# Padding the activation slots and weight ring of a hybrid decoder layer so that matmul operands start in many alignments

## The chip, the cores and the metric

The kernel runs on one core of a Trainium2 chip. The time is the device time of one execution of the whole layer, in microseconds. Before the change the median of two runs was 1518.17 us (1517.32 to 1519.03).

## What is computed

One layer of a decoder for 256 tokens with 2048 features, all in float32. Cut to what matters:

```python
def hybrid_mixer(h, w_in, mla_q_norm, mla_w_q_up, mla_kv_norm, mla_w_kv_up,
                 swa_sinks, rel_table, w_o_mla, w_o_swa, w_out):
    c_q, c_kv, k_r, q_s, k_s, v_s, gates = jnp.split(h @ w_in, offsets, axis=-1)
    q = (rms_norm(c_q, mla_q_norm) @ mla_w_q_up).reshape(B, S, MLA_HEADS, MLA_NOPE_DIM + MLA_ROPE_DIM)
    kv = (rms_norm(c_kv, mla_kv_norm) @ mla_w_kv_up).reshape(B, S, MLA_HEADS, MLA_NOPE_DIM + MLA_V_DIM)
    ...
    o_a = mla_attention(q[..., :MLA_NOPE_DIM], q_rope, kv[..., :MLA_NOPE_DIM], k_rope, kv[..., MLA_NOPE_DIM:])
    o_b = swa_attention(q_s, k_s, v_s, swa_sinks, rel_table)
    g = jax.nn.sigmoid(gates.astype(jnp.float32)).reshape(B, S, N_BRANCHES, D_MODEL)
    merged = g[:, :, 0] * (o_a @ w_o_mla).astype(jnp.float32) + g[:, :, 1] * (o_b @ w_o_swa).astype(jnp.float32)
    return merged.astype(h.dtype) @ w_out

def reference(x, ...):
    h = rms_norm(x, norm_mix_pre[l])
    y = hybrid_mixer(h, w_in[l], ...)
    x = x + rms_norm(y, norm_mix_post[l])
    h = rms_norm(x, norm_ffn_pre[l])
    y = conv_ffn(h, ffn_w_up[l], ffn_conv_w[l], ffn_conv_b[l], ffn_w_down[l])
    return x + rms_norm(y, norm_ffn_post[l])
```

`conv_ffn` multiplies by `w_up` (2048 x 11264), runs a causal convolution of width 3 and a gated GELU, and multiplies by `w_down` (5632 x 2048). Most of the work is in the large products with w_in (2048 rows, 7488 columns), w_o_mla, w_o_swa, w_out, w_up and w_down.

## The kernel before

**Splitting into high and low parts.** Each float32 factor is stored as two float32r parts, high and low, whose sum is the number. A product takes three matmuls (`mm3`, lines 142 to 145): high activation with high weight, high with low, low with high. The activation is the stationary operand (128 x 128, loaded into the array), the weight is the moving one (up to 512 columns that stream past it).

**Large products** go through `gemm` (lines 147 to 173). It keeps two accumulators of 128 tokens x 512 columns in PSUM and walks over the rows of the weight, in chunks of two tiles of 128 rows (1024 numbers a partition; for 320 columns also two tiles, for 256 four). `wchunk` (lines 101 to 120) fetches a chunk: SyncE issues the load into a raw buffer (three in the ring), ScalarE writes its high part (line 118), VectorE subtracts and writes the low part (line 119). The ring has five buffers for high parts and five for low parts, of 1024 numbers, 4096 bytes a partition. For some chunks `own` gives another pool (`px`, `p8`) in place of the ring, at the seams of the W_out and FFN stages. So for each chunk of two row tiles and each of two token tiles TensorE runs three matmuls: twelve of 512 columns.

**Activation slots.** Transposed activations lie in slots of 512 numbers (2048 bytes a partition): a pair of row tiles, each with 256 tokens. `slot_a` and `slot_b` (lines 92 and 93) name 16 slots each in the pool `base`: ah0 to ah7 and al0 to al7, bh0 to bh7 and bl0 to bl7. `pair_view` (line 95) picks row tile k: slot k // 2, and 256 numbers from its half. The a slots hold first the normed input (products with w_in), then the merged branches (w_out), then eight of the twelve gated FFN pairs (w_down); the b slots hold the sliding-window output (w_o_swa), the latent-attention output (w_o_mla), and the normed FFN input (w_up). The remaining four FFN pairs, gh8 to gh11 and gl8 to gl11, are tiles of the pool `p7` (line 876).

**Where things lie.** Pools lie one behind the other in a partition; each tile starts at a multiple of 32 bytes. In `base` come the constants, the a slots, seven small tiles of the input norm (ssx, v1, r1s, rh, r1_y, r1_t, r1_u), the b slots, eight small tiles of the latents' norms; then the ring with its raw, high and low buffers; then the pools of the stages.

**Order of the work.** Attention and the convolution run in small steps (`at`, `tick`) that are emitted between the chunks of the large products. Except in the first product, a scheduler in the framework sets the order on each engine; the change touches none of it.

Of the kernel before, what the change touches and what calls it, by code (L numbers as in the profile page):

```python
# [12 lines left out]
F32R = mybir.dt.float32r  # L13
# [28 lines left out]
def trunk_layer(ctx, tc, x, g_mix_pre, g_mix_post, g_ffn_pre, g_ffn_post, w_in, g_q, w_q, g_kv, w_kv,  # L42
# [16 lines left out]
    def sb(pl, shape, name, dt=F32, tag=None, bufs=None):  # L59
        return pl.tile(shape, dt, name=name, tag=tag or name, **({"bufs": bufs} if bufs else {}))  # L60

# [1 line left out]
    ident = sb(base, [P, P], "ident")  # L63
    make_identity(nc, ident)
    ident_r = sb(base, [P, P], "ident_r", F32R)
# [22 lines left out]
    rtab = sb(base, [P, NT, 4, 64], "rtab")  # L88
    sink = sb(base, [P, SH], "sink")

    # activations, transposed, as high and low float32r parts
    slot_a = lambda p, part: sb(base, [P, 512], f"a{part}{p}", F32R)
    slot_b = lambda p, part: sb(base, [P, 512], f"b{part}{p}", F32R)

    def pair_view(tiles):
        return lambda k: tiles[k // 2][:, (k % 2) * 256:(k % 2) * 256 + 256]

# [1 line left out]
    cnt = [0]  # L99

    def wchunk(src, shape, own=None, rawp=None):
        i = cnt[0]
        cnt[0] += 1
        n = int(np.prod(shape))
        raw = rawp.tile([P, 1024], F32, name=f"raw{i}", tag="xraw") if rawp else \
            ring.tile([P, 1024], F32, name=f"raw{i}", tag="raw", bufs=RAW)
        dst = raw[:, :n]
        if len(shape) == 2:
            dst = dst.rearrange("p (a b) -> p a b", a=shape[0])
        elif len(shape) == 3:  # L110
            dst = dst.rearrange("p (a b c) -> p a b c", a=shape[0], b=shape[1])
        if len(shape) == 3:
            for k in range(shape[0]):
                nc.sync.dma_start(dst[:, k], src[:, k])
        else:
            nc.sync.dma_start(dst, src)
        hi, lo = ((own or ring).tile([P, 1024], F32R, name=f"w{part}{i}", tag="w" + part) for part in ("hi", "lo"))
        act.copy(hi[:, :n], raw[:, :n])  # L118
        vec.tensor_tensor(lo[:, :n], raw[:, :n], hi[:, :n].bitcast(F32), op=ALU.subtract)  # L119
        return hi, lo  # L120

    # side work, in small steps that are emitted between the chunks of the large products
    steps = defaultdict(list)
    now = [0]

# [19 lines left out]
        pe.matmul(o, al, bh, start=False, stop=stop)  # L145

    def gemm(xh, xl, w, k0, nk, c0, n, split=False, pre=None, extra=None):
        """tokens x n columns of (activation rows k0.. of w); split: all of token tile 0 first."""
        kc = 1024 // n if n in (256, 512) else 2
        acc = new_acc("g")  # L150
        todo = []
        cuts = [0, 1, 2] + list(range(4, nk + 1, 2)) if pre else list(range(0, nk, kc)) + [nk]
        for ci, (k, ke) in enumerate(zip(cuts[:-1], cuts[1:])):
            kk = ke - k
            src = w[(k0 + k) * P:(k0 + k + kk) * P, c0:c0 + n].rearrange("(a p) n -> p a n", p=P)
            if pre and ci == 0:
                pre(k, ke)
            hi, lo = wchunk(src, [kk, n], *(extra or {}).get(ci, ()))
            if pre and ke < nk:
                pre(ke, cuts[ci + 2])  # L160
            for j in range(kk):
                kt = k + j
                wh, wl = hi[:, j * n:(j + 1) * n], lo[:, j * n:(j + 1) * n]
                for t in range(NT):
                    def go(kt=kt, t=t, wh=wh, wl=wl):
                        mm3(acc[t][:, :n], xh(k0 + kt)[:, t * P:(t + 1) * P],
                            xl(k0 + kt)[:, t * P:(t + 1) * P], wh, wl, kt == 0, kt == nk - 1)
                    if split and t == 1:
                        todo.append(go)
                    else:  # L170
                        go()
            tick()
        return acc, todo

    def rsqrt(v, n, name, pl):
        y = sb(pl, [P, n], f"{name}_y")
        t = sb(pl, [P, n], f"{name}_t")
        u = sb(pl, [P, n], f"{name}_u")
        vec.tensor_scalar(y.bitcast(I32), v.bitcast(I32), -0.5, float(0x5F3759DF), op0=ALU.mult, op1=ALU.add)
        def vyy():  # L180
            if n == 1:
                vec.scalar_tensor_tensor(t, v, y[:, 0:1], y, op0=ALU.mult, op1=ALU.mult)
            else:
                vec.tensor_tensor(t, y, y, op=ALU.mult)
                vec.tensor_tensor(t, t, v, op=ALU.mult)

        # a step of second order, then one of third order
        vyy()
        vec.tensor_scalar(t, t, -0.5, 1.5, op0=ALU.mult, op1=ALU.add)
        vec.tensor_tensor(y, y, t, op=ALU.mult)  # L190
        vyy()
        vec.tensor_scalar(u, t, 0.375, -1.25, op0=ALU.mult, op1=ALU.add)
        vec.tensor_tensor(u, u, t, op=ALU.mult)
        vec.scalar_tensor_tensor(y, u, 1.875, y, op0=ALU.add, op1=ALU.mult)
        return y

    def split_to(hi, lo, src, scale=None):
        """hi + lo = src * scale exactly; src in PSUM or SBUF, scale a number or a [P, 1] column."""
        if scale is None:
            act.copy(hi, src)  # L200
            vec.tensor_tensor(lo, src, hi.bitcast(F32), op=ALU.subtract)
        else:
            act.activation(hi, src, AF.Copy, scale=scale)
            vec.scalar_tensor_tensor(lo, src, scale, hi.bitcast(F32), op0=ALU.mult, op1=ALU.subtract)

# [1 line left out]
    esl, lpool = open_pool("lpool")  # L207
    es0, p0 = open_pool("p0")
    grow = sb(p0, [16, P], "grow")
# [53 lines left out]
    rh = sb(base, [P, NT], "rh")  # L263
    junk = sb(p0, [P, 512], "junk", tag="junk", bufs=2)

    # T5 bias of each head along the distance, with the mask beyond the window
    strip = dram.tile([SH, 384], F32, name="strip")
    relx = sb(lpool, [33, SH], "relx")
    pool.memset(relx[32:33, :], 1.0)
# [24 lines left out]
    r1 = x_norm()  # L294
    es0.close()

# [1 line left out]
    # keys and values run backwards within their blocks, so that the bias is strip[q + column]  # L298
    es1, p1 = open_pool("p1")
    kx = [sb(p1, [P, 2, 384], f"kx{g}", F32R) for g in range(4)]  # L300
    vx = [sb(p1, [P, 4, 2, 64], f"vx{t}", F32R) for t in range(NT)]
# [34 lines left out]
    qx_of, xs_of = {}, {}  # L336

    def swa_q(g, acc):
        """8 heads' queries, high parts beside low parts"""
        qx_of[g] = []  # L340
        for t in range(NT):
            q = sb(p1, [P, 8, 2, 64], f"qx{g}_{t}", F32R, tag="qx", bufs=2)
            a3 = acc[t].rearrange("p (a b) -> p a b", b=64)
            split_to(q[:, :, 0, :], q[:, :, 1, :], a3, r1s[:, t:t + 1])
            qx_of[g].append(q)

    def swa_qT(u):
        """queries of heads 2u, 2u + 1, transposed: high parts above low parts"""
        qx, i = qx_of[u // 4], u % 4
        pt = pst.tile([P, 512], F32R, name=f"xp{u}", tag="t")  # L350
        for j in range(2):
# [5 lines left out]
        xs_of[u] = xt  # L357

    def p_transpose(p, dst, tag):
        """probabilities [q0k0 | q1k0 | q1k1] of a head, transposed: [q1k1 | q0k0 | q1k0]"""  # L360
        pt = pst.tile([P, 512], F32, name=f"pt{tag}", tag="t")
        for j, c in enumerate((2, 0, 1)):
            pe.transpose(pt[:, j * P:(j + 1) * P], p[:, c * P:(c + 1) * P], ident)  # L363
        split_to(dst[0], dst[1], pt[:, 0:384])

    def swa_unit(u, t0):
        """heads 2u, 2u + 1, from step t0 on"""
        g = u // 4
        h0 = 2 * u
        st = {}  # L370
# [51 lines left out]
            p_transpose(st["p"][:, i, :], [w_[:, i, :] for w_ in st["pt"]], f"{u}_{i}")  # L422

        def pv():
            """high V above low V, against the probabilities' high and low parts of both heads"""
            st["po"] = pst.tile([P, 512], F32, name=f"po{u}", tag="t")
            st["o"] = sb(p1, [P, 256], f"o{u}", tag="o", bufs=2)
            v0, v1 = (vx[t][:, g, :, :].rearrange("p a b -> p (a b)") for t in range(NT))
# [25 lines left out]
            at(b + 1 + i // 2, lambda u=4 * g + i: swa_qT(u))  # L454
            swa_unit(4 * g + i, b + 2 + 2 * i)

# [1 line left out]
    cqh = [sb(lpool, [P, 512], f"cqh{i}", F32R) for i in range(2)]  # L458
    cql = [sb(lpool, [P, 512], f"cql{i}", F32R) for i in range(2)]
    ckh = sb(lpool, [P, 512], "ckh", F32R)  # L460
# [26 lines left out]
        return nrm, tr  # L487

    def rope(dst, src, tmp, t, which, nh):
        """dst = rope(src); src, dst [P, nh, 64], tables [cos | cos] and [-sin | sin]"""  # L490
        c = rtab[:, t, which, :]
        s = rtab[:, t, which + 1, :]
        b = lambda ap, n: ap.unsqueeze(1).to_broadcast([P, nh, n]) if nh > 1 else ap.unsqueeze(1)
# [28 lines left out]
    at(now[0] + 2, k_rope)  # L522
    at(now[0] + 3, lambda tr=tr: tr(0))

# [1 line left out]
    ta_d = dram.tile([4, NT, P, 512], F32, name="ta_d")  # L526
    yb_d = dram.tile([4, NT, P, 512], F32, name="yb_d")

# [16 lines left out]
    drain()  # L545
    es1.close()

# [1 line left out]
    es2, p2 = open_pool("p2")  # L549
    CQH, CQL = pair_view(cqh), pair_view(cql)  # L550
    CKH, CKL = pair_view([ckh]), pair_view([ckl])
# [3 lines left out]
    xr_of = {}  # L555

    def q_rope4(f, t0):
        """rope queries of heads 4f.., transposed, high above low, from step t0 on"""
        st = {}

        def mms(t):
# [28 lines left out]
        at(t0 + 4, lambda: tr(1))  # L590

    def mla_unit(u, t0):
        """heads 2u, 2u + 1, from step t0 on"""
        h0 = 2 * u
        st = {}

# [113 lines left out]
    es2.close()  # L710
    esl.close()

# [1 line left out]
    es3, p3 = open_pool("p3")  # L714
    mth = [slot_a(p, "h") for p in range(8)]
    mtl = [slot_a(p, "l") for p in range(8)]
# [34 lines left out]
        for p in range(2):  # L751
            at(now[0] + 1 + p, lambda p=2 * j + p, ld=ld: m_cols(p, ld))

# [1 line left out]
    gpost = sb(p6, [P, D], "gpost", tag="gp")  # L755
    pool.dma_start(gpost, g_mix_post.partition_broadcast(P))
    yg = [[sb(p6, [P, 512], f"yg_{t}_{j}", tag="f" + "ab"[t], bufs=4) for j in range(4)] for t in range(NT)]
# [64 lines left out]
            for t in range(NT):  # L822
                y_evac(acc, b, t)

# [1 line left out]
    first_extra = {0: (p8,)} | {i + 1: (px,) for i in range(EXTRA)}  # L826
    first_extra[EXTRA + 2] = (None, p8)
    resid(1)
# [1 line left out]
    GH, GL = pair_view(gT[0]), pair_view(gT[1])  # L830

    def conv_cols(sa, k, i, slot):
        """conv, gelu and gate of channels 128k.., into ktile slot"""
        w0, w1, w2, cb_ = (cvT[:, 44 * q + k:44 * q + k + 1] for q in range(4))
        pt = pst.tile([P, 512], F32, name=f"fT{k}", tag="t")
        for q in range(2):
# [14 lines left out]
        split_to(GH(slot), GL(slot), uu)  # L851

    def ffn_up(c, slot0, first=False):
        """channels 512c.., into ktiles slot0.."""
        sa = [[None, None], [None, None]]

        def evac(acc, q):
# [136 lines left out]
```

## Time and profile before

| | |
|---|---|
| median of two runs | 1518.17 us |
| profiled execution, first to last instruction | 1515.5 us |
| difference between the two | 2.7 us |
| TensorE matmuls | 7347, busy 1496.3 us |
| weight loads into the array (PEld) | 7347, busy 1246.4 us |
| VectorE busy | 940.8 us |
| ScalarE busy | 800.4 us |
| bytes moved by DMA | 285.46 MB, mean 188 GB/s |

Busy times of one engine can overlap those of another. PE is the matmul itself, PEld the load of its stationary operand, which runs beside the matmul before it. A matmul's recorded duration includes the passage through the array and overlaps the next one, so a mean duration of 390 ns does not mean one matmul every 390 ns; the time from start to start gives the pace. In a row of the groups stand line, engine, operation, output and inputs (moving first, stationary second), shape, count, then busy time in us and mean ns of one, then idle time before them.

### The profile page before, as it was taken

How to read it: one execution, taken by the hardware profiler on the slowest of the kernel's cores; microseconds unless marked ns; L12 is line 12 of the kernel's file. 1: busy time of each engine (PE TensorE's matmuls, PEld its weight loads, DVE VectorE, ACT ScalarE, POOL GpSimd, SP SyncE). 2: the span in 40 equal slices, each digit the busy share in tenths (PEclk: the TensorE clock that was granted, in tenths of full speed). 3: DMA queues.
4: the chain of work that ended last, by engine and by line, in shares of the span. 5: the costliest groups of instructions: out<-in, count | busy, mean ns of one | idle time of the engine just before them, and what ended most of it. 6: DMA issues, size and time to landing. Idle time of an engine off the chain costs nothing.

```text
span 1515.5 us, 20149 instructions
## 1 busy us (share of the span) xinstructions
PE 1496.3 (99%) x7347; PEld 1246.4 (82%) x7347; DVE 940.8 (62%) x1607; ACT 800.4 (53%) x1289; POOL 66.8 (4%) x114
## 2 busy tenths in 40 slices
PE   8999999999999999999999999999999999999997
PEld 6888878888898887888788888888888888888887
DVE  5688884444666764565676666666544476666755
ACT  6588874344555553444565555555434455555542
POOL 2122200000000002000000000000000000000000
PEclk9999999999999999999999999999999999999999
DMA  7776556666655558765655665555566655665553
GB/s 236 215 177 164 164 162 182 208 203 207 181 152 168 162 160 292 254 217 185 199 174 179 196 190 183 184 183 186 185 193 189 193 185 178 189 192 182 179 194 113
DMA packets 160803, 285.46 MB, mean 188 GB/s; under 512 B 18419, under 2 KB 33893, under 8 KB 160448
## 3 DMA queue, kind: packets, MB, share of 16 engines
q1 hardware_dynamic: 154736, 264.81, 55.2%
q0 software_dynamic: 5968, 19.36, 5.0%
q8 instruction: 58, 0.95, 0.2%
q14 instruction: 41, 0.34, 0.1%
HBM read 277.79 MB, written 6.34 MB: 187 GB/s over the span
## 4 chain that ended last, share of the span: by engine, by line
PE 92%; DVE 2%; DMA 2%; ACT 2%; issue 1%; SPq 0%; DVEq 0%; ACTq 0%
PE accg L143 27%; PE accg L145 27%; PE accg L144 27%; DMA raw<-in_w_in_dram 2%; PE fT L838 1%; DVE wlo L119 1%; DMA raw<-in_w_o_mla_dram 1%; PE mpo L679 1%; PE ms L645 1%; ACT whi L118 1%; PE qn L610 1%; PE qn L609 1%; PE qn L608 1%; ACT p L405 0%; PE pt L363 0%
## 5 line engine op out<-in xcount | busy, mean ns | idle before, releaser
L119 DVE TENSOR_TENSOR wlo<-raw,whi 128x1024 fp32r<-128x1024 f32 (+2 forms) x501 | 609.1, 1217 | 496.5 <-ACT whi L118 495.9
L118 ACT CAST whi<-raw 128x1024 fp32r<-128x1024 f32 (+2 forms) x501 | 522.9, 1045 | 603.8 <-PE accg L145 512.6
L143 PE MATMUL accg<-whi,bh 128*128 128x512 f32 x960 | 378.1, 394 | 0.0
L145 PE MATMUL accg<-whi,bl 128*128 128x512 f32 x960 | 374.4, 390 | 0.0
L144 PE MATMUL accg<-wlo,bh 128*128 128x512 f32 x960 | 373.7, 389 | 0.0
L143 PE MATMUL accg<-whi,ah 128*128 128x512 f32 (+2 forms) x896 | 348.7, 390 | 0.4 <-ACT whi L118 0.4
L144 PE MATMUL accg<-wlo,ah 128*128 128x512 f32 (+2 forms) x896 | 345.8, 386 | 0.5 <-DVE wlo L119 0.5
L145 PE MATMUL accg<-whi,al 128*128 128x512 f32 (+2 forms) x896 | 344.8, 385 | 0.0
L145 PEld LDWEIGHTS accg<-whi,bl 128*128 128x128 f32 x960 | 180.2, 188 | 38.5
L144 PEld LDWEIGHTS accg<-wlo,bh 128*128 128x128 f32 x960 | 180.4, 188 | 36.1
L143 PEld LDWEIGHTS accg<-whi,bh 128*128 128x128 f32 x960 | 180.3, 188 | 35.7
L145 PEld LDWEIGHTS accg<-whi,al 128*128 128x128 f32 x896 | 168.7, 188 | 35.6
L144 PEld LDWEIGHTS accg<-wlo,ah 128*128 128x128 f32 x896 | 168.8, 188 | 34.4 <-DVE wlo L119 1.6
L143 PEld LDWEIGHTS accg<-whi,ah 128*128 128x128 f32 x896 | 168.8, 189 | 33.4 <-ACT whi L118 1.3
L143 PE MATMUL accg<-whi,gh 128*128 128x512 f32 (+1 forms) x104 | 39.2, 377 | 0.0
L144 PE MATMUL accg<-wlo,gh 128*128 128x512 f32 (+1 forms) x104 | 38.8, 373 | 0.0
L145 PE MATMUL accg<-whi,gl 128*128 128x512 f32 (+1 forms) x104 | 38.4, 374 | 0.0
L405 ACT ACTIVATE p<-p,nm 128x128 f32<-128x128 f32 x64 | 28.3, 445 | 5.8 <-DVE nm L396 5.8
L838 PEld LDWEIGHTS fT<-ident,f 128*128 128x128 f32 x176 | 21.8, 139 | 5.8
L838 PE MATMUL fT<-ident,f 128*128 128x128 f32 x176 | 26.3, 272 | 0.0
L842 ACT ACTIVATE cc<-fT,cvT 128x256 f32<-128x256 f32 x44 | 24.2, 550 | 0.0
L143 PEld LDWEIGHTS accg<-whi,gh 128*128 128x128 f32 x104 | 19.6, 188 | 4.1 <-ACT gh L200 0.8
(304 smaller groups left out, 1284.7 us busy)
## 6 DMA issues: line engine op xcount, KB each, us to landing
raw<-in_ffn_w_up_dram SPq DMA_DIRECT2D x176, 512.0 KB, 4.0
raw<-in_w_in_dram SPq DMA_DIRECT2D x111, 512.0 KB, 4.4
raw<-in_ffn_w_down_dram SPq DMA_DIRECT2D x88, 512.0 KB, 3.7
raw<-in_w_o_swa_dram SPq DMA_DIRECT2D x32, 512.0 KB, 3.7
raw<-in_w_o_mla_dram SPq DMA_DIRECT2D x32, 512.0 KB, 4.6
raw<-in_w_out_dram SPq DMA_DIRECT2D x32, 512.0 KB, 3.7
raw<-in_mla_w_q_up_dram SPq DMA_DIRECT2D x48, 128.0 KB, 2.6
bias<-strip POOLq DMA_DIRECT2D x16, 256.0 KB, 4.1
```

What stands on the lines that cost most here:

```text
L118: act.copy(hi[:, :n], raw[:, :n])
L119: vec.tensor_tensor(lo[:, :n], raw[:, :n], hi[:, :n].bitcast(F32), op=ALU.subtract)
L143: pe.matmul(o, ah, bh, start=start, stop=False)
L144: pe.matmul(o, ah, bl, start=False, stop=False)
L145: pe.matmul(o, al, bh, start=False, stop=stop)
L405: act.activation(pb[:, i, a:b], pb[:, i, a:b], AF.Exp, bias=st["nm"][:, i, t:t + 1], accum_out=st["sm"][:, i, t:t + 1])
L608: pe.matmul(o, wh, ch(k), start=k == 0, stop=False)
L609: pe.matmul(o, wh, cl(k), start=False, stop=False)
L610: pe.matmul(o, wl, ch(k), start=False, stop=k == nk - 1)
L645: pe.matmul(o, w, v_, start=n == 0, stop=False)
L838: pe.transpose(pt[:, q * 256 + t * P:q * 256 + (t + 1) * P], sa[t][q][:, i * P:(i + 1) * P], ident)
L842: act.activation(cc, a, AF.Identity, scale=w2, bias=cb_)
```

## The change

The slots are allocated 8 numbers (32 bytes) wider, and the program uses 512 numbers of them: in the high slots from the start, in the low slots from number 4, 16 bytes in. High and low chunks of the ring are allocated 8 numbers wider and their first 1024 are used; chunks with a pool of their own stay as they are. So the slots and ring chunks behind each other start 2080 and 4128 bytes apart, where it was 2048 and 4096. Comments and docstrings are dropped; the number of instructions, their shapes and their order in the source are the same.

```diff
-    # activations, transposed, as high and low float32r parts
-    slot_a = lambda p, part: sb(base, [P, 512], f"a{part}{p}", F32R)
-    slot_b = lambda p, part: sb(base, [P, 512], f"b{part}{p}", F32R)
+
+
+    def slot(name, p, part):
+        o = 4 if part == "l" else 0
+        return sb(base, [P, 512 + 8], f"{name}{part}{p}", F32R)[:, o:o + 512]
+
+    slot_a = lambda p, part: slot("a", p, part)
+    slot_b = lambda p, part: slot("b", p, part)
...
-        hi, lo = ((own or ring).tile([P, 1024], F32R, name=f"w{part}{i}", tag="w" + part) for part in ("hi", "lo"))
+        hi, lo = ((own or ring).tile([P, 1024 + (0 if own else 8)], F32R, name=f"w{part}{i}", tag="w" + part)[:, 0:1024]
+                  for part in ("hi", "lo"))
```

## The prediction

> **What bounds the kernel now.** I read the page first: busy shares, the clock by slices, the chain that ended last.
>
> ```profile
> span 1515.5 us, 20149 instructions
> PE 1496.3 (99%) x7347; PEld 1246.4 (82%) x7347; DVE 940.8 (62%) x1607; ACT 800.4 (53%) x1289; POOL 66.8 (4%) x114
> ...
> PEclk9999999999999999999999999999999999999999
> ...
> PE 92%; DVE 2%; DMA 2%; ACT 2%; issue 1%; SPq 0%; DVEq 0%; ACTq 0%
> ...
> raw<-in_ffn_w_up_dram SPq DMA_DIRECT2D x176, 512.0 KB, 4.0
> ```
>
> TensorE is busy for 99% of the span, its clock is granted in full everywhere, and 92% of the chain is matmuls. Then I read the waits, to see whether anything feeds TensorE late.
>
> ```profile
> ACT whi L118 <- PE accg L145: 512.6, 335, 3.5
> DVE wlo L119 <- ACT whi L118: 495.9, 389, 4.2
> ...
> ACT whi L118 <- DMA raw<-in_w_o_mla_dram: 27.2, 14, 4.3
> ```
>
> ScalarE, which writes the high part of each weight chunk, waits 512.6 us for matmuls that give a ring chunk back; for a load it waits a twentieth of that. The ring is full most of the time. So the bound is the pace at which one matmul follows another. Next I read the groups by form, for how many matmuls there are of which size.
>
> ```profile
> L143 PE MATMUL accg<-whi,bh 128*128 128x512 f32 x960 | 378.1, 394 | 0.0
> L145 PE MATMUL accg<-whi,bl 128*128 128x512 f32 x960 | 374.4, 390 | 0.0
> L144 PE MATMUL accg<-wlo,bh 128*128 128x512 f32 x960 | 373.7, 389 | 0.0
> L143 PE MATMUL accg<-whi,ah 128*128 128x512 f32 x800 | 320.6, 401 | 0.4 <-ACT whi L118 0.4
> L144 PE MATMUL accg<-wlo,ah 128*128 128x512 f32 x800 | 317.7, 397 | 0.5 <-DVE wlo L119 0.5
> L145 PE MATMUL accg<-whi,al 128*128 128x512 f32 x800 | 316.8, 396 | 0.0
> ...
> L143 PE MATMUL accg<-whi,gh 128*128 128x512 f32 x88 | 34.7, 395 | 0.0
> L144 PE MATMUL accg<-wlo,gh 128*128 128x512 f32 x88 | 34.3, 390 | 0.0
> L145 PE MATMUL accg<-whi,gl 128*128 128x512 f32 x88 | 33.9, 391 | 0.0
> ```
>
> There are 3 x (960 + 800 + 88) = 5544 matmuls of 512 columns. The surprise is the mean: 401, 397, 396 ns with the a slots as stationary operand, but 394, 390, 389 with the b slots. Instruction, line, size and weights are the same; 7 ns lie between them. A duration here includes a pipeline that overlaps the next matmul, so I took the pace from stretches in which all matmuls are of one kind: first W_out (a slots), then a stretch late in the FFN (the last g tiles, then b slots). In both, the count includes one matmul that began before the stretch.
>
> ```profile
> 680.00:750.00 70.00, 70.00 (x301) 1.00 0.61 197
> 1157.00:1215.00 58.00, 58.00 (x257) 1.00 0.60 191
> ```
>
> The pace is 70.00 / 300 = 233.3 ns with a and 58.00 / 256 = 226.6 ns with b. With 3 x 800 = 2400 matmuls of the first kind and 3144 of the second, the terms are 2400 x 233.3 = 559.9 us and 3144 x 226.6 = 712.4 us, together 1272.3 us of the 1515.5.
>
> **What differs between a and b** is only where they start. Adding up the tiles of the code in their order, each rounded up to 32 bytes: the a slots start at a multiple of 64 bytes; seven small tiles (ssx to r1_u, 224 bytes) lie before the b slots, so these start 32 past such a multiple; so do the ring's chunks (eight more small tiles and three raw chunks between) and the last g tiles. Moving and stationary operand start in the same phase of 64 bytes at 226.6 ns, in opposite phases at 233.3. The two explanations, that the relation of the two decides or that the stationary start alone does, can't be told apart in this trace.
>
> Smaller matmuls show no such difference. Here are the first and last of 96 with a slots at 256 columns, the first and last of 12 with g tiles, and the first and last of 19 with a slots at 320 columns:
>
> ```profile
> 1477.78 0.28 PE L143 MATMUL accg<-whi,ah 128*128 128x256 f32 x1
> ...
> 1489.02 0.28 PE L145 MATMUL accg<-whi,al 128*128 128x256 f32 x1
> ```
> ```profile
> 1497.68 0.28 PE L143 MATMUL accg<-whi,gh 128*128 128x256 f32 x1
> ...
> 1498.99 0.28 PE L145 MATMUL accg<-whi,gl 128*128 128x256 f32 x1
> ```
> ```profile
> 199.19 0.31 PE L145 MATMUL accg<-whi,al 128*128 128x320 f32 x1
> ...
> 201.83 0.31 PE L145 MATMUL accg<-whi,al 128*128 128x320 f32 x1
> ```
>
> ```profile
> L144 PE MATMUL accg<-wlo,ah 128*128 128x256 f32 x64 | 18.0, 281 | 0.0
> ```
>
> The starts give 11.24 / 95 = 118.3 ns, 1.31 / 11 = 119.1 ns and 2.64 / 18 = 146.7 ns; the last fence is the group of the first form. So for matmuls of 256 and 320 columns I take no change.
>
> After a break the b pace needs some matmuls to settle. Here a group of transposes went before:
>
> ```profile
> 1010.05 0.47 PE L143 MATMUL accg<-whi,bh 128*128 128x512 f32 x1
> 1010.37 0.39 PE L144 MATMUL accg<-wlo,bh 128*128 128x512 f32 x1
> 1010.59 0.39 PE L145 MATMUL accg<-whi,bl 128*128 128x512 f32 x1
> 1010.82 0.40 PE L143 MATMUL accg<-whi,bh 128*128 128x512 f32 x1
> 1011.06 0.39 PE L144 MATMUL accg<-wlo,bh 128*128 128x512 f32 x1
> 1011.28 0.40 PE L145 MATMUL accg<-whi,bl 128*128 128x512 f32 x1
> 1011.52 0.39 PE L143 MATMUL accg<-whi,bh 128*128 128x512 f32 x1
> 1011.75 0.39 PE L144 MATMUL accg<-wlo,bh 128*128 128x512 f32 x1
> ```
>
> From 1010.37 to 1011.75 six intervals take 1.38 us, 230 ns each, single ones between 220 and 240. The settled 226.6 is thus a state into which equal alignments fall when they repeat; it is not what each matmul costs by itself.
>
> **The change part by part.** Instructions: none is added, removed or moved. The slots become 520 columns wide (2080 bytes) and the ring's high and low chunks 1032 (4128 bytes), and slices of the old size are used. Memory grows by 32 x 32 + 10 x 32 = 1344 bytes a partition, a multiple of 64, so the pools behind the ring keep their phase of 64 bytes, and so do the raw chunks that the loads land in.
>
> Starts after the change, modulo 64: the high part of slot p alternates between 0 and 32, the low part between 16 and 48, in a and in b alike (the 16 a slots widen by 512 bytes in all). Of five high ring chunks three start at 32 and two at 0; the low chunks begin 5 x 4128 bytes later, so of them three start at 0 and two at 32. The three matmuls of a product take high, low, high weights: the moving operand is at 0 in (2 x 0.4 + 0.6) / 3 = 47% of them. The stationary operand is at 0 or 32 in two thirds and at 16 or 48 in one third. Only 0.67 x 0.53 = 36% of the matmuls, 1970, keep a pair that this trace shows; 3574 get one that it doesn't.
>
> Cost of an unknown pair, from both sides: the nearest rows are the settled paces 226.6 and 233.3, 6.7 ns apart. An unknown pair could lie as far outside them as they lie apart: 220 ns or 240 ns. I take a value between, because neighbours now differ at nearly every matmul: slots change every second row tile, weights alternate from high to low. The settled state of b should be gone, and what remains is an unsettled pace: 230 ns as b shows it after a break, 233.3 where the phases are opposite; their middle is 231.6. A second route gives the same: from 256 to 320 columns the pace grows by 28.4 ns, 0.444 ns a column, and 192 columns more make 146.7 + 85.2 = 231.9. I take 231.5 for all 5544: 1283.4 us against 1272.3, **+11 us**. Some of the b matmuls are in unsettled stretches today and lose nothing, so I round to **+10 us**.
>
> ScalarE and VectorE write the same elements, some 16 bytes further on.
>
> ```profile
> L119 DVE TENSOR_TENSOR wlo<-raw,whi 128x1024 fp32r<-128x1024 f32 x491 | 601.2, 1226 | 494.7 <-ACT whi L118 494.1
> L118 ACT CAST whi<-raw 128x1024 fp32r<-128x1024 f32 x491 | 515.9, 1052 | 601.3 <-PE accg L145 512.0 <-DMA raw<-in_w_o_mla_dram 27.2 <-DMA raw<-in_w_in_dram 18.6
> ```
>
> A chunk feeds 12 matmuls of 512 columns, some 2.8 us; VectorE needs 1.23 us of that and ScalarE 1.05. I cost their writes at nothing: the full ring hides them. Without that cover a tenth more on both would be (601.2 + 515.9) / 10 = 112 us, but it would first have to use up 1.5 us in every chunk.
>
> The sum: the profiled execution spans 1515.5 us, 2.7 under the median of 1518.2 of the runs, so I add the change to both: 1525.5 us of span and **1528 us** as time. About 2% either way, 1488 to 1548, is what a measurement of this kernel can tell from no change.
>
> **The rivals.** *Low parts cost more (slower).* A stationary operand that starts 16 bytes off a multiple of 32 appears nowhere in the trace. If its load takes a step more, it touches the matmul it belongs to and the one during which it is loaded, two thirds of all, 3696. At 240 ns these add 3696 x 8.5 = 31 us to my sum: 1559 us. If one third is touched, 1544. It decides from a mean pace of 1272.3 + 30.4 over 5544, 235 ns. For it: phase costs something at all, and 16 bytes is a finer fault than any in the trace. Against: weights load beside the matmul before (PEld is busy 82% and the chain doesn't name it).
>
> *An aligned moving operand is cheap (faster).* All moving operands now start 32 past a multiple of 64, so each reads a half block first and last. If those 47% (2589) that start at 0 run at 220 ns, they save 2589 x 11.5 = 30 us of my sum: 1498 us; if all 3574 unknown pairs do, 1487 us. For it: no operand pair in the trace is free of the offset. Against: at 256 columns nothing depends on phase.
> The Trainium skill (TensorE: Matmul & The Clock Gate, Back-to-back issue gap) has some 216 ns for 512 columns at full clock; the trace disagrees, with 226.6 ns at best, and if that gap came back the sum would be lower still by its figure.
>
> *Nothing changes.* If the mean pace over many pairs is today's 1272.3 / 5544 = 229.5 ns, the time stays 1518 us: half the pairs with opposite phases and half with equal ones would give 230.0 ns, 1521.
> The Trainium skill (SBUF — State Buffer, Specifications) says that memory lines are 16 bytes and that crossing to a new line costs; every start here, before and after, is a multiple of 16, so by that rule nothing changes, and a and b should already be equal. The trace disagrees with it: 233.3 against 226.6 ns.
>
> **How the numbers follow.** My forecast, the unsettled pace, gets 0.48 and spans 1520 to 1538. Nothing changes: 0.14. Cheap aligned operand: 0.17, of which 0.08 below 1488. Costly low parts: 0.21, of which 0.18 above 1548. So faster 0.08, within 2% 0.74, slower 0.18. The range reaches from the first case of the fast rival, 1498, to nearly the full price of the slow one, 1556.
>
> **What would show it.** Right: in the W_out stretch and in the late FFN stretch the counts come to one pace near 231.5 ns, a and b durations by form meet around 394 ns, nothing differs between high and low parts, and the forms with 256 columns keep 281 ns. Wrong: line 145 (low stationary part), or line 143 that follows, stands out by over 5 ns; or the pace falls under 226.6, or alternates with the ring chunk. Also wrong would be new waits of matmuls for ScalarE or VectorE.

## The result, and the profile after

| | before | after |
|---|---|---|
| median of two runs | 1518.17 us | 1526.44 us (1525.41 to 1527.47) |
| profiled execution, its time | | 1525.41 us |
| profiled execution, its span | 1515.5 us | 1523.6 us |

The ratio of the times is 1.007, with a 95% interval of 1.0046 to 1.0095: slower by 0.7%, within the 2%. The forecast was 1528 us, +10 where +8.3 came; the interval of the ratio stands for 7 to 14 us, so the measurement does not tell the two apart. One execution of experiment 3 below ran at a granted clock of 0.75, took 1846 us and is left out of its median; all others had 0.996 or more.

First the page of the changed kernel: span, busy times, granted clock, the chain that ended last.

```profile
span 1523.6 us, 20149 instructions
PE 1508.2 (99%) x7347; PEld 1246.6 (82%) x7347; DVE 940.2 (62%) x1607; ACT 799.1 (52%) x1289; POOL 66.8 (4%) x114
...
PEclk9999999999999999999999999999999999999999
...
PE 93%; DVE 2%; DMA 2%; ACT 2%; issue 1%; SPq 0%; DVEq 0%; ACTq 0%
```

The instructions are the same, the clock is granted in full in every slice, and VectorE and ScalarE are as busy as before to within 1.3 us. TensorE alone has 11.9 us more of busy time. Next the waits of the weight chunks (lines are 6 further on than before: 124 and 125 write a chunk, 149 to 151 are the three matmuls).

```profile
ACT whi L124 <- PE accg L151: 514.3, 330, 2.4
DVE wlo L125 <- ACT whi L124: 505.7, 386, 5.1
```

ScalarE still waits half a millisecond for matmuls to give a chunk back: the ring is full, and the writers of the padded tiles cost nothing. The groups by form, as before:

```profile
L149 PE MATMUL accg<-whi,bh 128*128 128x512 f32 x960 | 382.3, 398 | 0.0
L151 PE MATMUL accg<-whi,bl 128*128 128x512 f32 x960 | 378.5, 394 | 0.0
L150 PE MATMUL accg<-wlo,bh 128*128 128x512 f32 x960 | 378.1, 394 | 0.0
L149 PE MATMUL accg<-whi,ah 128*128 128x512 f32 x800 | 319.7, 400 | 0.0
L150 PE MATMUL accg<-wlo,ah 128*128 128x512 f32 x800 | 316.5, 396 | 0.1
L151 PE MATMUL accg<-whi,al 128*128 128x512 f32 x800 | 315.9, 395 | 0.0
...
L150 PE MATMUL accg<-wlo,ah 128*128 128x256 f32 x64 | 17.9, 280 | 0.0
```

The b forms rose from 394, 390, 389 ns to 398, 394, 394; the a forms fell by one each, from 401, 397, 396. The form with 256 columns kept its 281 ns to within one. And the pace, in the same two stretches (the W_out products with a slots, and late in the FFN the last g tiles and then b slots):

```profile
680.00:750.00 70.00, 70.00 (x303) 1.00 0.62 191
1162.00:1220.00 58.00, 58.00 (x251) 1.00 0.63 184
```

One matmul of each count began before its stretch: 70.00 / 302 = 231.8 ns and 58.00 / 250 = 232.0 ns, where it was 233.3 and 226.6. The two paces have become one.

### The profile page after: what moved, and what is told of

It is laid out like the page before. It is cut to its first block, busy times and chain, and to the rows that moved or that the text cites. A ratio compares the mean times of both kernels' runs of the same rounds, so it can differ in the third digit from the quotient of the medians.

```text
span 1523.6 us, 20149 instructions
## 1 busy us (share of the span) xinstructions
PE 1508.2 (99%) x7347; PEld 1246.6 (82%) x7347; DVE 940.2 (62%) x1607; ACT 799.1 (52%) x1289; POOL 66.8 (4%) x114
## 4 chain that ended last, share of the span: by engine, by line
PE 93%; DVE 2%; DMA 2%; ACT 2%; issue 1%; SPq 0%; DVEq 0%; ACTq 0%
PE accg L149 28%; PE accg L151 28%; PE accg L150 28%; DMA raw<-in_w_in_dram 1%; PE fT L844 1%; PE mpo L685 1%; DMA raw<-in_w_o_mla_dram 1%; DVE wlo L125 1%; PE ms L651 1%; ACT whi L124 1%; PE qn L616 0%; PE qn L614 0%; PE qn L615 0%; ACT p L411 0%; PE pt L369 0%
## 5 line engine op out<-in xcount | busy, mean ns | idle before, releaser
L149 PE MATMUL accg<-whi,bh 128*128 128x512 f32 x960 | 382.3, 398 | 0.0
L151 PE MATMUL accg<-whi,bl 128*128 128x512 f32 x960 | 378.5, 394 | 0.0
L150 PE MATMUL accg<-wlo,bh 128*128 128x512 f32 x960 | 378.1, 394 | 0.0
```

The source lines that it names most:

```text
L149: pe.matmul(o, ah, bh, start=start, stop=False)
L150: pe.matmul(o, ah, bl, start=False, stop=False)
```

## The experiments

The theory, T: what counts is the **relation** of the starts of the moving and the stationary operand within a block of memory; equal phases run at 226.7 ns, opposite ones at 233.3 (both after some matmuls of one kind), and a relation that changes from matmul to matmul lies between, near 232. Its rivals, by the letters of the expectations: S, the start of the stationary operand alone sets the pace; A, a moving operand that starts at a multiple of 64 bytes is cheap by itself; P, each pair of starts has a price of its own, and a sequence costs the mean of its pairs; L, only the phase in steps of 32 bytes counts, so the low parts' 16 bytes cost nothing. Every kernel below is an edit of the kernel before, and computes all of it; the time of the kernel before stands beside each, from the same chip. Times are medians, ratios have their 95% intervals. A long group is an unbroken run of 36 or more matmuls of 512 columns with a or b slots; each kernel has 30. Its pace is taken from start to start, from the fifteenth matmul to the last.

The places are shifted by lengthening small tiles that lie ahead of a group of tiles: `cvT` lies ahead of all slots, `rh` between the a and the b slots, `ck_ss` between the b slots and the ring. Counted from the start of the program's memory, the a slots of before start 128 bytes past a multiple of 256, the b slots, the ring and the last g tiles 96 past one.

**1. All starts equal, at a multiple of 64 (e1_all0).** One tile is 32 bytes longer:

```diff
-    rh = sb(base, [P, NT], "rh")
+    rh = sb(base, [P, 16], "rh")[:, 0:NT]
```

> The tile rh is 32 bytes longer, nothing else: the b slots, the ring and all behind move by 32 bytes, so every slot, ring chunk and last g tile now starts at a multiple of 64. Theory T (equal phases that repeat settle at 226.6 ns, opposite ones at 233.3, the place itself does not matter): the a slots join the b slots at 226.6 ns, group means 389 to 394 ns, 2400 x 6.7 = 16 us less than before, 1502 us. Rival S (the stationary start alone decides, 32 past a multiple of 64 is fast): all 5544 at 233.3 ns, group means 396 to 401, 3144 x 6.7 = 21 us more, 1539 us. Rival A (an aligned moving operand is cheap): under 226.6 ns, at 220 some 1466 us.

Measured: 1504.02 us against 1515.74, ratio 0.9927 (0.9912 to 0.9942). The groups by form of this kernel, and the W_out stretch:

```profile
L143 PE MATMUL accg<-whi,bh 128*128 128x512 f32 x960 | 378.3, 394 | 0.0
...
L143 PE MATMUL accg<-whi,ah 128*128 128x512 f32 x800 | 316.4, 396 | 0.0
L144 PE MATMUL accg<-wlo,ah 128*128 128x512 f32 x800 | 313.3, 392 | 0.5 <-DVE wlo L119 0.5
L145 PE MATMUL accg<-whi,al 128*128 128x512 f32 x800 | 312.9, 391 | 0.0
```
```profile
680.00:740.00 60.00, 60.00 (x266) 1.00 0.65 200
```

The a matmuls fell to nearly the durations of b, and 60.00 / 265 is 226.4 ns where the a slots ran at 233.3. Nothing but a start in memory has moved. S is wrong: the a slots' own start is the same as before. The gain is 11.7 us and not 16, for the a matmuls too now have to settle after each break: from start to start they average 228.2 ns (530.9 us in 2327 intervals of the trace), where 233.1 was their mean before.

**2. All starts equal, 32 bytes further on (e2_all32).** As 1, and `cvT` 184 columns long with 176 used.

> cvT and rh are 32 bytes longer each: the a slots move by 32 bytes, all behind by 64, so every slot, ring chunk and last g tile starts 32 past a multiple of 64. T and S both say 226.6 ns everywhere, 1502 us. If this is slower or faster than the run with all starts at a multiple of 64, the absolute start counts too (rival A: the other one is faster).

Measured: 1503.96 us against 1515.74, the same ratio to four places. Whether all start at a multiple of 64 or 32 past one makes no difference, as long as they start alike. A, the aligned moving operand, is wrong.

**3. Opposite everywhere (e3_opposite).** As 2, and `ck_ss` 32 bytes longer: a and b slots lie 32 bytes from the ring's phase.

> cvT, rh and ck_ss are 32 bytes longer each: all a and b slots start 32 past a multiple of 64, ring chunks and the last g tiles at one. T: a and b slots at 233.3 ns, the 264 matmuls with the last g tiles at 226.6; 2880 x 6.7 = 19 us more than before, 1537 us. S: a and b at 226.6, the last g tiles at 233.3; (2400 - 264) x 6.7 = 14 us less, 1504 us.

Measured: 1530.66 us against 1515.74, ratio 1.0104 (1.0086 to 1.0121). The timeline of this kernel, first and last of 119 matmuls in a row with b slots:

```profile
831.64 0.39 PE L144 MATMUL accg<-wlo,bh 128*128 128x512 f32 x1
...
859.17 0.39 PE L145 MATMUL accg<-whi,bl 128*128 128x512 f32 x1
```

The same 119 matmuls of experiment 1:

```profile
818.04 0.39 PE L144 MATMUL accg<-wlo,bh 128*128 128x512 f32 x1
...
844.81 0.39 PE L145 MATMUL accg<-whi,bl 128*128 128x512 f32 x1
```

27.53 / 118 = 233.3 ns against 26.77 / 118 = 226.9 ns. The b slots have got the pace that only a slots had: T holds, its 19 us came as 15. From 0.7% faster than the kernel before to 1.0% slower, and nothing but starts in memory moved.

**4 and 5. Each half of the change alone.** In e4_ring_only the ring chunks are 1032 columns, as in the change, and the slots are as before; in e5_slots_only the slots are 520 columns, with the low parts at the start, and the ring is as before.

```diff
-        hi, lo = ((own or ring).tile([P, 1024], F32R, name=f"w{part}{i}", tag="w" + part) for part in ("hi", "lo"))
+        hi, lo = ((own or ring).tile([P, 1024 + (0 if own else 8)], F32R, name=f"w{part}{i}", tag="w" + part)[:, 0:1024]
+                  for part in ("hi", "lo"))
```

> Only the ring chunks of the change: 4128 bytes apart, slots as before. T: the moving operand's phase changes at nearly every matmul, so nothing settles: about 232 ns for a and b alike, group means 394 to 395, 1526 us, as with the whole change. S: stationary starts are as before, so 233.3 for a and 226.6 for b, 1518 us.

> Only the slots' padding of the change, without the 16 bytes of the low parts: slots 2080 bytes apart, so neighbours alternate between a multiple of 64 and 32 past it; ring as before, 32 past. The stationary phase now changes every second row tile, once in 12 matmuls, and stays equal or opposite to the moving one for 12 matmuls. T (a state is reached after about seven matmuls of one kind): half of the matmuls head for 226.6 and half for 233.3 and few settle; 231 ns in the mean, 1524 us. Rival P (each pair has its price, whatever came before): half at 226.6, half at 233.3 with sharp steps, 230.0 ns, 1518 us.

Measured: 1525.11 us against 1515.74, ratio 1.0063 (1.0047 to 1.0080), and 1524.71 against 1515.01, ratio 1.0062 (1.0047 to 1.0077). Either half alone costs what the whole change costs; the halves don't add. The groups of e4_ring_only meet as in the whole change:

```profile
L144 PE MATMUL accg<-whi,bh 128*128 128x512 f32 x960 | 382.4, 398 | 0.0
L146 PE MATMUL accg<-whi,bl 128*128 128x512 f32 x960 | 379.4, 395 | 0.0
...
L145 PE MATMUL accg<-wlo,ah 128*128 128x512 f32 x800 | 316.4, 395 | 0.0
L146 PE MATMUL accg<-whi,al 128*128 128x512 f32 x800 | 316.3, 395 | 0.0
```

In e4_ring_only the relation changes at most matmuls, and by the start times even those whose operands start alike within 256 bytes average 230.9 ns, not 226.7: there a matmul's cost depends on its neighbours, against P.

In e5_slots_only the relation lasts for twelve matmuls, and there the steps are sharp, as P said. I sorted the runs of twelve by the relation of their starts within 256 bytes. With equal starts the first eleven intervals take 226.8 ns in the mean, from the first one on; no seven matmuls are needed to reach that. With the weights' start 64 bytes past the slots' it is 230 ns, 64 bytes before it 234, so the direction counts too; the other five relations average 232 to 234. Six of eight relations thus cost about 233 ns, and the mean is 232 where P with two prices made it 230. So T's number came by another way than T's, and that is luck.

**6 and 9. How large the block is.** In e6_half128 slots and ring lie 64 bytes apart (`rh` as in 1, `ck_ss` 24 columns long), in e9_half256 128 bytes apart (`ck_ss` 40 columns). If a block of 64 bytes decided, both would run as experiment 1.

> As the run with all starts at a multiple of 64, but with ck_ss 64 bytes longer: slots start at a multiple of 128, ring chunks 64 past one. If only the phase within 64 bytes counts: 226.6 ns, 1504 us, the same as that run. If it is the phase within 128 bytes: above, up to 233.3 ns, 1531 us.

> As the run with all starts at a multiple of 64, but with ck_ss 128 bytes longer, so that slots and ring chunks lie 128 bytes apart within 256. If the phase repeats after 128 bytes: settled at 226.7 ns, 1504 us. If it goes on to 256: another settled pace, 228 to 233 ns, 1511 to 1532 us.

Measured: 64 apart 1512.81 us against 1515.01, ratio 0.9985 (0.9975 to 0.9995); 128 apart 1529.5 against 1516.27, ratio 1.0087 (1.0072 to 1.0103). The timeline of e6_half128, first and last of the same 119:

```profile
825.25 0.40 PE L144 MATMUL accg<-wlo,bh 128*128 128x512 f32 x1
...
852.27 0.39 PE L145 MATMUL accg<-whi,bl 128*128 128x512 f32 x1
```

And the W_out stretch of e9_half256:

```profile
680.00:740.00 60.00, 60.00 (x259) 1.00 0.64 200
```

27.02 / 118 = 229.0 ns at 64 bytes, a third settled pace (228.9 in every long group). At 128 bytes 60.00 / 258 = 232.6 ns by the count; by the start times ten of the long groups, W_out among them, run at about 233.3 ns and twenty at about 232.4. So a difference of 64 or 128 counts, and my block of 64 bytes was too small. The period is thus at least 256 bytes; experiment 11 tells whether it is more.

**7. A fixed sequence of phases (e7_low_weights_32).** `rh` as in 1, and a tile of 32 bytes between the high and the low chunks of the ring, so that the moving operand's phase goes 0, 32, 0 in each product, always the same.

```diff
+        if i == 0:
+            ring.tile([P, 8], F32R, name="gap", tag="gap", bufs=1)
```

> As the run with all starts at a multiple of 64, but a gap of 32 bytes in the ring lies between high and low chunks: low chunks start 32 past a multiple of 64, in a fixed round of three (moving 0, 32, 0; stationary always 0). P: two of three at 226.6, one at 233.3, mean 228.9 ns, 1509 us. T: the round repeats, but its neighbours differ, so equal phases never follow each other three times; unsettled, 232 ns, 1526 us; a settled round of three with one sum is possible too, somewhere between.

Measured: 1527.43 us against 1515.01, ratio 1.0079 (1.0064 to 1.0094). P is wrong: two thirds of these matmuls are in equal phase. The groups:

```profile
L147 PE MATMUL accg<-wlo,bh 128*128 128x512 f32 x960 | 382.9, 399 | 0.0
L146 PE MATMUL accg<-whi,bh 128*128 128x512 f32 x960 | 382.3, 398 | 0.0
L148 PE MATMUL accg<-whi,bl 128*128 128x512 f32 x960 | 376.0, 392 | 0.0
```

The third matmul is near its old 390, the first two pay. By the start times this kernel does settle, into rounds of three such as 231, 237, 226 ns, with a mean of 231.1, or in other groups 233.3 ns: a fixed mixture has settled paces too, only slower ones. T had named a settled round as possible, but had put its time at unsettled matmuls.

**8. The low parts' 16 bytes alone (e8_low_slots_16).** The low slots are cut from one tile, 16 bytes in; everything else starts equal, as in 1 (`ck_ss`, 64 columns long, brings the ring back to the slots' phase).

```diff
+        if p == 0:
+            big[name, part] = sb(base, [P, 8 * 512 + 8], f"{name}{part}", F32R)
+        return big[name, part][:, 4 + 512 * p:4 + 512 * (p + 1)]
```

> As the run with all starts at a multiple of 64, but the low activation parts start 16 bytes past one (the eight low slots of a or b are cut out of one tile). It is the 16 bytes of the change alone. T: one of three stationary operands has another phase, so the pace does not settle: 230 to 232 ns, 1518 to 1526 us. Rival L (the 16 bytes do not count, only the 32-byte phase does): 226.6 ns, 1504 us. Rival from the prediction (a load 16 bytes off costs more): line of the low activation part and the one after it stand out by over 5 ns.

Measured: 1520.74 us against 1515.01, ratio 1.0041 (1.0024 to 1.0057), but 16.7 us above experiment 1, from which only this differs. The groups:

```profile
L152 PE MATMUL accg<-whi,bh 128*128 128x512 f32 x960 | 381.3, 397 | 0.0
L153 PE MATMUL accg<-wlo,bh 128*128 128x512 f32 x960 | 379.0, 395 | 0.0
L154 PE MATMUL accg<-whi,bl 128*128 128x512 f32 x960 | 377.9, 394 | 0.0
```

L is wrong: it said 1504 us. The prediction's dearer load of the low part is wrong too, for its line (154) is the fastest of the three; a third of the operands at another phase slows all three. By the start times this kernel settles as well, which T had not said: 25 of the long groups run at about 232.2 ns, and five at 226.7, the pace of equal starts.

**10. All slots 16 bytes in (e10_all_slots_16).** High and low slots alike are cut as in 8, from tiles 256 bytes longer than their slots, and `rh` is as in 1: every pair is 16 bytes apart.

> As the run with all starts at a multiple of 64, but all slots of a and b, high and low, start 16 bytes past one (each eight cut out of one tile). The alignment is the same at every matmul, so it settles. If 16 bytes count half as much as 32: some 230 ns, 1518 us. If only steps of 32 bytes count: 226.7 ns, 1504 us. If a stationary operand 16 bytes off costs more than one 32 off: over 233.3 ns, more than 1532 us.

Measured: 1521.03 us against 1516.27, ratio 1.0037 (1.0023 to 1.0051), and a wide spread: ten executions between 1517.74 and 1525.73. The timeline of this kernel shows why. First and last of 119 matmuls in a row:

```profile
826.18 0.40 PE L153 MATMUL accg<-wlo,bh 128*128 128x512 f32 x1
...
853.72 0.40 PE L154 MATMUL accg<-whi,bl 128*128 128x512 f32 x1
...
872.60 0.39 PE L153 MATMUL accg<-wlo,bh 128*128 128x512 f32 x1
...
899.35 0.39 PE L154 MATMUL accg<-whi,bl 128*128 128x512 f32 x1
```

27.54 / 118 = 233.4 ns, and in the next long group, with the same instructions and phases, 26.75 / 118 = 226.7 ns. At 16 bytes apart the matmuls fall after a break into one settled state or the other and stay in it until the next break. In this execution twenty of the long groups run at 233.3 ns and ten at 226.7. That another share of the two makes another time, and so the spread, is likely, but only one execution was traced; what chooses is open.

**11. Padding without a change of phase (e11_pad_256).** As 1, and the high ring chunks 256 bytes longer.

> As the run with all starts at a multiple of 64, but the high ring chunks are padded by 256 bytes (4352 apart in place of 4096), so that the ring is padded and no phase within 256 bytes changes. If the phase is all that the padding changes: 226.7 ns, 1504 us. If the padding as such (the distance of the chunks, the later pools moved) costs: towards the 1525 us of the ring padded by 32 bytes.

Measured: 1503.3 us against 1514.38, ratio 0.9934 (0.9918 to 0.9951): the time of experiment 1. The groups:

```profile
L144 PE MATMUL accg<-whi,bh 128*128 128x512 f32 x960 | 378.1, 394 | 0.0
...
L145 PE MATMUL accg<-wlo,ah 128*128 128x512 f32 x800 | 313.5, 392 | 0.3 <-DVE wlo L120 0.3
```

Padding costs nothing by itself, and an offset of 256 bytes or a multiple of it between neighbours isn't felt. With 6 and 9 this makes the period 256 bytes, as far as these distances tell.

This is also the best version: one tile 32 bytes longer makes the kernel 0.7% faster than before, and by the two ratios, 0.9927 / 1.007, about 1.4% faster than the change.

## Why the prediction was right, point by point

**The bound** was right: full clock as recorded (but for 3.4 us of the kernel before, see the terms), full ring, no new wait of a matmul for ScalarE or VectorE. Their writes cost nothing, as said.

**The mechanism**, settled paces that give way to one unsettled pace near 231.5 ns, was right: 231.8 and 232.0 in the two stretches, in a and b alike, with 394 ns foreseen and 394 to 400 measured by form. In the changed kernel the long groups run anywhere between 231.2 and 233.0 ns, and the 450 matmuls of unbroken runs whose operands still start alike within 256 bytes average 232.2 ns from start to start, where all average 232.1: the fast state is gone for them too. Experiments 1 to 3 decided what the trace of before had left open: the relation of the two starts, not the stationary start alone.

That 231.5 lies so close is partly luck. The middle of 230 and 233.3 was a choice within 220 to 240, the second route was a straight line through two smaller sizes, and experiment 5 comes to 232 by another way.

**The terms.** I added up the intervals from start to start of both traces by what the stationary operand is; intervals of over 0.30 us after a matmul of 512 columns count as breaks.

| | before, us | after, us | measured | predicted |
|---|---|---|---|---|
| 512 columns, b slots | 643.9 | 657.2 | +13.3 | 2880 x 4.9 = +14.1 |
| 512 columns, last g tiles | 59.0 | 60.1 | +1.1 | 264 x 4.9 = +1.3 |
| 512 columns, a slots | 540.6 | 539.5 | -1.1 | 2400 x -1.8 = -4.3 |
| breaks (134, then 129) | 50.4 | 45.5 | -4.9 | 0 |
| all else | 210.1 | 209.8 | -0.2 | 0 |

The sum is +8.2, the span's growth +8.1. The predicted +10 was off by 2 for two errors of opposite sign. The a slots win less: five of their intervals are no longer breaks and count here, and their mean is 232.1 ns, not 231.5. And breaks got shorter, which I had not looked at. The waits of TensorE in the kernel before, and below them in the changed one:

```profile
PE ckT L483 <- DVE ckl L204: 2.6, 1, 2.6
PE warm L73 <- DVE ident_b L68: 2.0, 1, 2.0
PE mT L731 <- DVE lta L750: 1.9, 2, 1.7
PE xt L255 <- DMA xc<-in_x_dram: 1.4, 2, 0.8
```
```profile
PE warm L73 <- DVE ident_b L68: 2.0, 1, 2.0
PE ckT L489 <- DVE ckl L210: 1.3, 1, 1.3
PE mT L737 <- DVE lta L756: 1.0, 2, 0.8
PE xt L261 <- DMA xc<-in_x_dram: 0.9, 1, 0.9
```

Two transposes that wait for VectorE's side work and one for a load wait 2.7 us less. That a slower TensorE leaves VectorE more time is only an argument: experiment 1, with a faster one, waits less than the kernel before too (1.7 us for ckT), so part of it differs from execution to execution.

I had overlooked one more thing in the trace of before. Behind the longest of these waits the granted clock fell to half for 3.4 us; in the changed kernel it stayed full in the same stretch:

```profile
226.90:230.31 3.41, 3.04 (x8) 0.50 0.87 281
```
```profile
226.90:230.31 3.41, 3.41 (x16) 1.00 0.90 294
```

In the kernel before, the six intervals there took 2.71 us (from 227.61 to 230.32), where six at 233.3 ns take 1.40. All six count as breaks, and their absence is why the changed kernel has five fewer; with the wait, this place (221 to 236 us) makes 3.7 of the 4.9 us. The prediction's "granted in full everywhere" missed it. The traces of experiments 4 and 6 have one such stretch each and that of experiment 8 two, so nothing ties it to the change.

**What the prediction put wrongly** is the working of the phases, "modulo 64". The period is 256 bytes, so the shares that I worked out (36% known pairs) are shares of something that doesn't decide. The price survived, because it did not come from them: with 256 bytes, too, almost every matmul has another phase than its neighbour. And "a state into which equal alignments fall when they repeat" is half of it: every relation that was held fixed has a settled pace or two (226.7 ns equal, 226.7 or 233.3 at 16 bytes, 233.3 at 32, 228.9 at 64, 232.4 or 233.3 at 128), short fixed rounds have them too (experiments 7 and 8), and a relation that lasts for twelve matmuls shows its price at once (experiment 5). Unsettled are the kernels whose weights change their phase from chunk to chunk.

**The rivals.** Nothing changes: outside the interval. Costly low parts: line 151 doesn't stand out (394 against 394 and 398), and experiment 8 has it fastest. Nor does the load itself take longer. Here are the loads of the low b parts before, after and in experiment 3; the last number is the idle time before them:

```profile
L145 PEld LDWEIGHTS accg<-whi,bl 128*128 128x128 f32 x960 | 180.2, 188 | 38.5
```
```profile
L151 PEld LDWEIGHTS accg<-whi,bl 128*128 128x128 f32 x960 | 180.2, 188 | 42.6
```
```profile
L145 PEld LDWEIGHTS accg<-whi,bl 128*128 128x128 f32 x960 | 180.1, 188 | 43.7
```

The cheap aligned operand: experiments 1 and 2 are equal. By the Trainium skill (SBUF — State Buffer, Specifications), memory lines are 16 bytes, and by that rule no kernel here should differ from another, since all starts are multiples of 16; the runs disagree, from 1503 to 1531 us.

**Open.** Why the relation of the starts matters at all. Whether the two operands get in each other's way while the next stationary one is loaded (PEld is busy 82%, beside the matmuls) wasn't tried: no run takes the loads away. Two things bear on it. The recorded loads last 188 ns at the slow pace as at the fast; what grows is the time between them. And in experiment 5 the step comes one interval early: the twelfth matmul of a run with equal starts, beside which the next slot's operand is loaded, takes 232.8 ns, and the twelfth of the run before one with equal starts 228.0. That points to the next stationary operand rather than the matmul's own, but the twelfth intervals of the other runs, 229 to 236 ns, follow no such order, so it isn't shown. And all of this is shown only for float32r, 512 columns, a new stationary operand for each matmul.

## What to carry to other kernels

Where matmul after matmul bounds a kernel, look at the pace from start to start in stretches of one kind: if two stretches with the same instruction differ by a few per cent, compare where their operands start, and bring moving and stationary tiles to the same start within 256 bytes. Keep tile sizes of such operands to multiples of 256 bytes, for then the relation of the first tiles holds for all; a small tile of odd length between two groups shifts everything behind it. Changes of a size somewhere ahead in memory can move a time by 1% with no instruction changed, so an experiment that alters a tile's size should keep the phases of the rest.

## What the runs showed of the hardware that I had not expected

A matmul of 512 columns has settled states: 226.7 and 233.4 ns for the same instructions in one execution (experiment 10). The step between them is (27.54 - 26.75) / 118 = 6.7 ns; by the start times, 226.7 is 34 such steps and 233.3 is 35, and the settled b matmuls of the kernel before keep to one grid of 6.67 ns through the whole execution, but for a drift of under 2 ns. It looks as if a matmul had to begin on a beat of something that runs freely; that is a guess, and what it would be, no run here shows.

After a break the fast pace takes some matmuls to come: in the long groups of experiment 1 the first six to nine intervals take 228 to 235 ns in the mean. Over its 2327 intervals with a slots the mean is 228.2 ns, 1.5 above the settled pace, or 3 us in all; that is part of why experiment 1 won 11.7 us and not 16.

The Trainium skill (TensorE: Matmul & The Clock Gate, Back-to-back issue gap) has some 216 ns for 512 columns as the gap of isolated matmuls, and 131 ns for a stream of loads and matmuls; the lowest settled pace of any run here, a stream of loads and matmuls, was 226.7 ns.
